# The first three projections on shared x tiles, one more kind of weight split by accumulation, and another order of the last head's value products

## The chip, the cores and the metric

The kernel runs on one core of a Trainium2 chip. The metric is the device time of one launch in microseconds (us). Three runs of the kernel before gave 1087.66, 1087.67 and 1087.76 us, so the median is 1087.67.

## What is computed

One layer of a hybrid encoder: x has 576 rows (512 of a prompt, 64 of a sample) and 1024 columns. A mixer with a gated delta rule and a gated linear attention (4 heads each), a cross attention of 4 heads into 256 memory tokens, and a feed-forward block with a causal convolution are added to x one after the other.

```python
def _mixer(h, p, l, conv_prev, s_a, s_b):
    proj = h @ p['w_in'][l]
    qkv, b_raw, a_raw, z_a, q_b, k_b, v_b, g_lr, z_b, gt_a, gt_b = _split_cols(proj, IN_SIZES)
    qkv, conv_new = _causal_dwconv(qkv, p['conv_a_w'][l], conv_prev)
    ...
    o_a, s_a_new = _gated_delta_chunked(q_a, k_a, v_a, g_a, beta, s_a.astype(f32))
    ...
    merged = jax.nn.sigmoid(gt_a) * y_a + jax.nn.sigmoid(gt_b) * y_b
    return merged @ p['w_o'][l], conv_new, s_a_new, s_b_new

def _cross_attn(h, k, v, w_q, w_o):
    q = (h @ w_q).reshape(B, L, MEM_HEADS, MEM_HD).astype(jnp.float32)
    s = jnp.einsum('blhd,bmhd->bhlm', q, k.astype(jnp.float32)) * (MEM_HD ** -0.5)
    a = jax.nn.softmax(s, axis=-1)
    o = jnp.einsum('bhlm,bmhd->blhd', a, v.astype(jnp.float32)).reshape(B, L, D_MODEL)
    return o.astype(h.dtype) @ w_o

def _trunk(...):
        x = x + _mixer(_rmsnorm(x, p['norm_mix'][l]), ...)
        x = x + _cross_attn(_rmsnorm(x, p['norm_mem'][l]), ...)
        x = x + _conv_ffn(_rmsnorm(x, p['norm_ffn'][l]), ...)
```

Everything is fp32. Outputs are the rows of both requests and the new states.

## The kernel before

**Tiles.** x lies transposed in 8 tiles of 128 features by 576 rows. A weight tile is 128x1024: a block of 128 output columns, its 8 parts of 128 input features side by side. To keep fp32 precision each operand is split into a high half and a low half (the difference), and one product is three matmul passes: high with high, high with low, low with high. `mm3` does this for one x tile: each pass has one matmul of 256 rows and one of 320, six in all. In traces `xh` and `xl` are halves of normed x, `w` holds a weight's halves, `wr` the raw weight as loaded, `ws` a sum of raw blocks, `sm` a PSUM bank.

**Two ways to split a weight.** Either ACT copies the high half (a CAST) and DVE or POOL subtracts to get the low half; or, for tiles called `summed`, ACT writes the negated high half into the low half's place (an ACTIVATE) and a DMA on POOL's queue adds the source to it in place (`w<-wt` from HBM, `w<-ws` from a sum in SBUF). Six weight tiles are in use at a time (three more in a later stage), and four raw ones.

**Products in seven.** The output projection `wo` (and some other weights) is done in pairs of column blocks with seven products for eight (P1, P2, P3, Q4 to Q7) of half-size blocks, each 12 matmuls of 288 columns. P1, P2 and Q4 use one block of the weight; Q5, Q6, P3 and Q7 use sums of blocks (s1 to s4), made by DVE or POOL. `emit_product` (L651) makes the weight of one product, and its flag `summed` (L688) selects the way of the split. After a product DVE adds the bank `sm` to x tiles (`x<-sm`), which frees the bank.

**Order.** Instructions are recorded by coroutines and a planner, class Driver (L251), issues them from one line, L292, engine by engine, by modelled ready times. `X` is a choice between DVE and POOL that the planner makes. So a change of one instruction's kind moves others.

**Start.** `main` (L1686) loads x tiles on SP's queue with the halves of the first weight tiles between them. `WPART` says behind which x tile a half of which raw tile comes. Weights 0 and 1 (q and k of head 0) are laid out together in HBM, so that each half holds both weights' parts for two x tiles. The loop over x tiles multiplies with q and, one tile behind, with k: 16 times `mm3`. Weight 2 (v of head 0) is loaded whole, split by accumulation, and its product follows later by `tile_proj`, after 32 small matmuls with `w` for the gates. Then comes z (`za`). `conv_raw` copies a product from PSUM to the tile u for the convolution.

**Attention.** `c_att` (L1527) does one head: probabilities, transposed and split (`pth`, `ptl`), then two value products of 128 columns each, both copied from PSUM to `ao` by ACT and split by `hl2` into `ach` and `acl`, which the `mo` products use. Between the two value products the coroutine waits for the first `ao`.

Of the kernel before, what the change touches and what calls it, by code (L numbers as in the profile page):

```python
# [10 lines left out]
F32 = mybir.dt.float32  # L11
# [6 lines left out]
P = 128  # L18
# [3 lines left out]
T = TP + TS  # L22
KT = D // P
# [5 lines left out]
RAWB = 4  # L29
# [474 lines left out]
def tile_trunk(ctx, tc, xT, memT, wt, wd, vec, cst, w0, wgate, st_gdn, st_conv, st_gla, st_ffn, ckT, cv,  # L504
# [19 lines left out]
    def nm(s):  # L524
        cnt[0] += 1
        return f"{s}{cnt[0]}"
# [30 lines left out]
    def big():  # L557
        return Pair(sm(), sm())
# [41 lines left out]
    def make(i):  # L600
        fn = unmade.pop(i, None)
        if fn is not None:
            fn()
# [8 lines left out]
    def emit_weight(i, at=0.0):  # L612
        kind, idx = WORDER[i]
        if kind == "*":
            wready[i] = emit_product(i, at, *idx)
            return
        raw = raw_tile()
        n = 1024
        if kind == "dn":
            m, p = idx  # L620
            n = len(PARTS[p]) * 128
            src = wd[m, :, PART0[p] * 128:PART0[p] * 128 + n]
        elif kind in ("outa", "outb"):
            n, c = 512, 512 * (kind == "outb")
            src = wt[WIDX[("out", idx)], :, c:c + 512]
        else:
            src = wt[WIDX[(kind, idx)]]
        DMA(raw[:, :n], src)
        h = w_tile()
        h, lo = (h[:, 0:512], h[:, 512:1024]) if n <= 512 else (h[:], w_tile()[:])  # L630
        summed = kind in SUMMED and (kind, idx) != ("dn", (7, 3))

        def split_():
            if summed:
                split_summed(h[:, :n], lo[:, :n], raw[:, :n], src)
            else:
                A.copy(h[:, :n], raw[:, :n])
                X.tensor_tensor(lo[:, :n], raw[:, :n], f(h[:, :n]), op=ALU.subtract)
            drop(raw[:])

        defer(i, split_, max(drv.ready_at(raw[:, :n]), at - (LEADD if summed else LEADV)))
        wready[i] = (h, lo)
# [8 lines left out]
    def emit_product(i, at, pair, prod):  # L651

        def dram(tile_):
            kind, idx = tile_
            if kind != "dn":
                return wt[WIDX[tile_]], 512
            m, p = idx
            n = len(PARTS[p]) * 64
            return wd[m, :, PART0[p] * 128:PART0[p] * 128 + 2 * n], n

        n = dram(pair[0])[1]
        u = used.setdefault(pair, set())
        if prod == "P1":
            r = halves_of[pair] = []
            for t_ in pair:
                raw = raw_tile()
                src, _ = dram(t_)
                DMA(raw[:, :2 * n], src)
                r += [(raw[:, 0:n], src[:, 0:n]), (raw[:, n:2 * n], src[:, n:2 * n])]
        r = halves_of[pair]  # L670
        (a11, d11), (a12, d12), (a21, _), (a22, d22) = r[:4]

        def total(a, b):
            s_ = slot("ws")
            (X if pair[0][0] in ("wo", "mo") else V).tensor_tensor(s_[:, 0:n], a, b, op=ALU.add)
            return s_[:, 0:n]

        def made(key, a, b):
            if key not in sums:
                sums[key] = total(a(), b())  # L680
            return sums[key]

        sums = sums_of.setdefault(pair, {})
        s1 = lambda: made("s1", lambda: a21, lambda: a22)
        s2 = lambda: made("s2", s1, lambda: a11)
        w = w_tile()
        h, lo = w[:, 0:n], w[:, 512:512 + n]
        summed = prod in ("P1", "P2", "Q4") or prod == "Q5" and n > 256 and pair[0][0] not in ("wo", "dn")  # L688

        def split_():  # L690
            src = {"P1": lambda: a11, "Q5": s1, "Q6": s2, "P3": lambda: made("s4", s2, lambda: a12),
                   "Q7": lambda: made("s3", lambda: a11, lambda: a21), "P2": lambda: a12, "Q4": lambda: a22}[prod]()
            if prod == "Q7":
                made("s4", s2, lambda: a12)
            if summed:
                split_summed(h, lo, src, {"P1": d11, "P2": d12, "Q4": d22}.get(prod, src))
            else:
                A.copy(h, src)
                X.tensor_tensor(lo, src, f(h), op=ALU.subtract)
            u.update({prod} | set(sums))  # L700
            for a, ps in ((a11, {"P1", "s2", "s3", "s4", "P2"}), (a22, {"s1", "s3", "Q4"})):
                if ps <= u:
                    drop(a)

        defer(i, split_, max(drv.ready_at(a11, a22) if prod not in ("P1", "P2") else drv.ready_at(a11), at - (LEADD if summed else LEADV)))
        return h, lo

    def weight(kind, idx, ahead=True, held=False):

        i = wpos[0]  # L710
        assert WORDER[i] == (kind, idx), (WORDER[i], kind, idx)
        wpos[0] = i + 1
        for j in [j for j in wready if j < i - held]:
            drop(*wready.pop(j))
        if i not in wready:
            emit_weight(i)
        make(i)
        if ahead:
            fetch(i + 1, i)
        return wready[i]  # L720
# [32 lines left out]
    cst_t = small_tile([P, NM - 256], F32, tag="cst", name="cst", bufs=1)  # L753
    DMA(vec_t[:, 0:8], vec[:, 0:8])
    x = []
    raws = [wp.tile([P, 1024], F32, tag="raw", name=nm("wr"), bufs=RAWB) for _ in range(2)]
    for t_ in raws:
        keep(drv.rotate("raw", RAWB, t_))

    WPART = {0: (0, 0, 512), 2: (0, 512, 1024), 3: (1, 0, 512), 5: (1, 512, 1024)}  # L760
    for k in range(KT):
        xt = slot("x")
        x.append(xt)
# [28 lines left out]
    def mm3(outs, wh, wl, a, b, k, first, last):  # L792
        ch = wh[:, k * 128:(k + 1) * 128]
        cl = wl[:, k * 128:(k + 1) * 128]
        for o, c in outs:
            PE.matmul(o, ch, a[:, c], start=first, stop=False)
        for o, c in outs:
            PE.matmul(o, ch, b[:, c], start=False, stop=False)
        for o, c in outs:
            PE.matmul(o, cl, a[:, c], start=False, stop=last)  # L800
# [726 lines left out]
    def c_att(hd):  # L1527
# [51 lines left out]
        for j in range(2):  # L1579
            pp, p64 = sm(), sm()  # L1580
            for mt_ in range(2):
                c = slice(256 * mt_ + 128 * j, 256 * mt_ + 128 * j + 128)
                vh_, vl_ = (t[:, c] for t in vp_)
                h, lo = (t[:, 0:TP] for t in pts[mt_])
                PE.matmul(pp, vh_, h, start=mt_ == 0, stop=False)
                PE.matmul(pp, vh_, lo, start=False, stop=False)
                PE.matmul(pp, vl_, h, start=False, stop=mt_ == 1)
                PE.matmul(p64[:, 0:64], vs_[:, c], pst[:, 64 * mt_:64 * mt_ + 64], start=mt_ == 0, stop=mt_ == 1)
            o = slot("ao")
            for c, reg in ((slice(0, TP), pp), (slice(TP, T), p64[:, 0:64])):  # L1590
                A.copy(o[:, c], reg)
            yield [o]
            ao[2 * hd + j] = hl2(o)
            os_.append(o)
            yield
        mops[hd] = {p: cut(ao[2 * hd + i], N1) for i, p in enumerate(("P1", "P2"))}
        drv.done.add(("att", hd))
# [16 lines left out]
    def hl2(src, new=None):  # L1614
        h, lo = [(new or slot)(s, F32R) for s in ("ach", "acl")]
        parts2(h[:, 0:T], lo[:, 0:T], src[:, 0:T])
        return h[:, 0:T], lo[:, 0:T]
# [71 lines left out]
    def main():  # L1689
        acc = slot("acc")  # L1690
        xg = []
        for i in range(2):
            wready[i] = (w_tile()[:], w_tile()[:])

        def wpart(k):
# [35 lines left out]
        DMA(keep_t, cst[:, 0:256])  # L1731
        DMA(cst_t, cst[:, 256:NM])
        drop(*(t_[:] for t_ in raws))
        emit_weight(2)
        make(2)
        DMA(wg_t, wgate)
        DMA(cst_in, st_conv)
        xs = xs_of(xg)
        b0 = []
        (wh0, wl0), (wh1, wl1) = weight("q", 0, False), weight("k", 0, True, True)  # L1740
        first2 = [big(), big()]
        for k in range(KT + 1):
            for i, ps in enumerate(first2):
                j = k - i
                if 0 <= j < KT:
                    wh, wl = (wh0, wl0) if j < 4 else (wh1, wl1)
                    mm3([(ps[:, 0, 0:256], slice(0, 256)), (ps[:, 1, 0:320], slice(256, T))], wh, wl, *xs[j], 2 * (j % 4) + i, j == 0, j == KT - 1)
        raw_u = [conv_raw(ps, V.tensor_copy) for ps in first2]
        for k in range(4, KT):
            sq_act(k)  # L1750
        drv.spawn(c_rstat("n1", [(acc, 0)], 4, True, 0.0))
# [20 lines left out]

        drv.spawn(c_first())

        yield from tile_proj("v", 0, xs, b0)
        u0 = conv_raw(b0[0], A.copy)
        yield from tile_proj("za", 0, xs, b0)
        z0 = slot("z")
        for i, o in pieces(b0[1], z0):
            A.copy(o, i)  # L1780
        yield ("first",)
        def c_gate_operands():
# [709 lines left out]
def pack_inputs(inp):  # L2492
# [13 lines left out]
    for (kind, idx), i in WIDX.items():  # L2506
# [11 lines left out]
        if (kind, idx) in HALVED:  # L2518
            w = np.concatenate([w.reshape(KT, P, P)[0::2], w.reshape(KT, P, P)[1::2]]).reshape(D, P)
        wt[i] = kp(w)  # L2520
    wt[0:2] = wt[0:2].reshape(2, P, 2, 4, P).transpose(2, 1, 3, 0, 4).reshape(2, P, 1024)
    wd = a["w_down"][0].reshape(NJ, P, 8, P)[sum(PARTK, [])].transpose(2, 1, 0, 3).reshape(8, P, NJ * P)

    w0 = np.zeros((D, 32), np.float32)
# [63 lines left out]
```

## Time and profile before

| what | value |
|---|---|
| median of three runs | 1087.67 us |
| the profiled execution, whole | 1090.06 us |
| its span, from the first to the last instruction | 1088.3 us |
| mean granted clock of TensorE | 0.997 |
| matmuls on PE | 8278 records |
| HBM read and written | 158.15 MB, 5.37 MB |

Nothing in this table says which work ends last; for that the page has a chain of work, and the trace has the waits of each engine. In a row of the timeline the first number is the start in us, then duration, engine, line, operation, output<-inputs, shapes and count; in brackets stands the idle time before it and what ended it. A duration of several instructions covers the stretch from the first one's start to the last one's end. A matmul's duration in the trace includes its passage through the array, so consecutive matmuls overlap, and the difference of starts is what one costs. PEld is the load of a weight into the array, which lies beside PE's matmuls. DMA-issuing rows on POOL last as long as the issue; the landing is in the views of the DMA issues.

### The profile page before, as it was taken

Reading aid. Unit: us, or ns where it says so; the run is one execution under the profiler, and the core shown is the slowest. Engines: PE = TensorE matmul, PEld = TensorE weight load, DVE = VectorE, ACT = ScalarE, POOL = GpSimd, SP = SyncE. Lnnn points to the kernel's source line nnn. Section 1 sums busy time; section 2 is a strip of 40 time slices with the busy share of each in tenths; the row PEclk is TensorE's granted clock in tenths of the full one; section 3 lists DMA queues with packets and bytes.
Section 4 is the critical chain, followed back from the end, with each engine's and each line's share of the span. In section 5 each row is a group of like instructions: output and inputs, shape, how many; then the busy total and the mean of one; then the engine's idle time right before and its main releaser. Section 6 shows DMA issues by size and latency. Waiting matters only on the chain.

```text
span 1088.3 us, 21600 instructions
## 1 busy us (share of the span) xinstructions
PE 1077.5 (99%) x8278; PEld 1045.7 (96%) x8278; DVE 749.4 (69%) x1460; ACT 705.9 (65%) x1404; POOL 363.3 (33%) x578
## 2 busy tenths in 40 slices
PE   9999999999999999999999999999999999999997
PEld 7999989998988999999999999999999999999997
DVE  6566844776757586887735766667877776778565
ACT  6675637464647568566755668768876776677645
POOL 1243216134524433123410125444333333332224
PEclk9999999999999999999999999999999999999999
DMA  9666344354136889678684258777788688778934
GB/s 295 145 143 162 70 110 114 76 123 122 43 78 130 213 213 188 246 222 211 174 221 146 49 124 195 175 166 150 166 195 196 146 213 188 168 172 184 201 77 112
DMA packets 68039, 172.00 MB, mean 158 GB/s; under 512 B 7904, under 2 KB 14176, under 8 KB 67936
## 3 DMA queue, kind: packets, MB, share of 16 engines
q0 software_dynamic: 30672, 71.84, 38.2%
q1 hardware_dynamic: 36976, 98.26, 27.7%
q8 instruction: 65, 1.06, 0.4%
q10 hardware_dynamic: 288, 0.52, 0.1%
q14 instruction: 38, 0.31, 0.1%
HBM read 158.15 MB, written 5.37 MB: 150 GB/s over the span
## 4 chain that ended last, share of the span: by engine, by line
PE 97%; DVE 1%; ACT 1%; DMA 0%; issue 0%; SPq 0%; ACTq 0%; DVEq 0%
PE sm L292 97%; DMA x<-xT 0%; DVE ql L292 0%; ACT w L292 0%; DVE w L292 0%; DVE acl L292 0%; DVE ws L292 0%; ACT ach L292 0%; SPq L292 0%; ACT ao L292 0%; DVE q L292 0%; DVE xl L292 0%; ACT xh L292 0%; DVE yo L292 0%; DVE x L292 0%
## 5 line engine op out<-in xcount | busy, mean ns | idle before, releaser
L292 PE MATMUL sm<-xh,w 128*128 128x290 f32 (+3 forms) x2304 | 446.3, 300 | 0.4 <-ACT xh L292 0.3
L292 PEld LDWEIGHTS sm<-xh,w 128*128 128x128 f32 x2304 | 357.2, 189 | 5.4 <-issue 1.7
L292 PE MATMUL sm<-xl,w 128*128 128x290 f32 (+3 forms) x1152 | 270.7, 296 | 0.5 <-DVE xl L292 0.5
L292 POOL DMA_DIRECT2D w<-wt x153 | 135.4, 898 | 372.4 <-ACT w L292 277.4
L292 PE MATMUL sm<-ach,w 128*128 128x256 f32 (+1 forms) x1216 | 230.9, 295 | 2.2 <-DVE x L292 1.7
L292 PEld LDWEIGHTS sm<-xl,w 128*128 128x128 f32 x1152 | 200.9, 189 | 1.0 <-DVE xl L292 1.0
L292 PEld LDWEIGHTS sm<-ach,w 128*128 128x128 f32 x1216 | 189.9, 188 | 3.0 <-ACT w L292 1.9
L292 ACT CAST w<-wr 128x512 fp32r<-128x512 f32 (+5 forms) x207 | 158.7, 769 | 20.8 <-PE sm L292 17.8
L292 ACT ACTIVATE w<-wr 128x512 fp32r<-128x512 f32 (+5 forms) x186 | 142.8, 769 | 20.4 <-PE sm L292 18.7
L292 PE MATMUL sm<-acl,w 128*128 128x256 f32 (+1 forms) x608 | 146.3, 295 | 0.3 <-DVE acl L292 0.3
L292 ACT CAST w<-ws 128x512 fp32r<-128x512 f32 (+1 forms) x132 | 78.4, 603 | 46.8 <-DVE ws L292 26.2
L292 PEld LDWEIGHTS sm<-acl,w 128*128 128x128 f32 x608 | 107.4, 188 | 0.5 <-DVE acl L292 0.5
L292 DVE TENSOR_TENSOR w<-ws,w 128x512 fp32r<-128x512 f32 (+1 forms) x104 | 76.1, 740 | 19.9 <-ACT w L292 17.7
L292 DVE SCALAR_TENSOR_TENSOR fc<-fu,vec,fc 128x578 f32<-128x578 f32 x88 | 70.4, 815 | 3.0 <-ACT fc L292 2.9
L292 PE MATMUL sm<-sh,w 128*128 128x290 f32 x288 | 61.2, 297 | 0.0
L292 DVE TENSOR_TENSOR x<-x,sm 128x320 f32<-128x320 f32 (+3 forms) x95 | 38.7, 437 | 31.4 <-PE sm L292 31.0
L292 POOL DMA_DIRECT2D w<-wd x33 | 29.0, 898 | 64.8 <-ACT w L292 57.9
L292 ACT ACTIVATE fc<-fu,vec 128x578 f32<-128x578 f32 x44 | 38.1, 871 | 17.0 <-POOL fu L292 16.4
L292 PEld LDWEIGHTS sm<-sh,w 128*128 128x128 f32 x288 | 47.5, 189 | 0.0
L292 DVE TENSOR_TENSOR ws<-ws,wr 128x512 f32<-128x512 f32 (+1 forms) x64 | 44.1, 690 | 1.1
L292 PE MATMUL sm<-oh,w 128*128 128x256 f32 (+1 forms) x256 | 44.7, 295 | 0.0
L292 POOL DMA_DIRECT2D w<-ws x27 | 23.6, 873 | 50.4 <-ACT w L292 49.9
(388 smaller groups left out, 1958.1 us busy)
## 6 DMA issues: line engine op xcount, KB each, us to landing
wr<-wt SPq DMA_DIRECT2D x130, 512.0 KB, 5.8
w<-wt POOLq DMA_DIRECT2D x52, 512.0 KB, 6.5
w<-wt POOLq DMA_DIRECT2D x101, 256.0 KB, 6.3
w<-ws POOLq DMA_DIRECT2D x27, 256.0 KB, 5.7
x<-xT SPq DMA_DIRECT2D x16, 288.0 KB, 6.1
wr<-wd SPq DMA_DIRECT2D x8, 448.0 KB, 5.9
w<-wd POOLq DMA_DIRECT2D x8, 448.0 KB, 7.1
wr<-wt SPq DMA_DIRECT2D x12, 256.0 KB, 3.8
```

What stands on the lines that cost most here:

```text
L292: fn(*args, **kw)
```

## The change

There are three edits. First, at the start v joins q and k: three raw tiles come in six halves behind x tiles 0, 1, 2, 3, 5 and 6, the three weights are laid out together in HBM with q, k and v of one x tile next to each other, and each x tile is multiplied with all three before the next. v's product is copied to u directly behind them. Second, `summed` holds also for Q5 of the `wo` pairs but the first, so three subtractions become ACTIVATEs with an accumulating DMA. Third, for head 3 the wait and the split between the two value products are dropped; both splits follow the second.

```diff
--- before.py
+++ after.py
@@ -685,7 +685,7 @@
         s2 = lambda: made("s2", s1, lambda: a11)
         w = w_tile()
         h, lo = w[:, 0:n], w[:, 512:512 + n]
-        summed = prod in ("P1", "P2", "Q4") or prod == "Q5" and n > 256 and pair[0][0] not in ("wo", "dn")
+        summed = prod in ("P1", "P2", "Q4") or prod == "Q5" and n > 256 and (pair[0][0] not in ("wo", "dn") or pair[0][0] == "wo" and pair[0][1])
 
         def split_():
             src = {"P1": lambda: a11, "Q5": s1, "Q6": s2, "P3": lambda: made("s4", s2, lambda: a12),
@@ -753,11 +753,11 @@
     cst_t = small_tile([P, NM - 256], F32, tag="cst", name="cst", bufs=1)
     DMA(vec_t[:, 0:8], vec[:, 0:8])
     x = []
-    raws = [wp.tile([P, 1024], F32, tag="raw", name=nm("wr"), bufs=RAWB) for _ in range(2)]
+    raws = [wp.tile([P, 1024], F32, tag="raw", name=nm("wr"), bufs=RAWB) for _ in range(3)]
     for t_ in raws:
         keep(drv.rotate("raw", RAWB, t_))
 
-    WPART = {0: (0, 0, 512), 2: (0, 512, 1024), 3: (1, 0, 512), 5: (1, 512, 1024)}
+    WPART = {k: (n // 2, 512 * (n % 2), 512 * (n % 2) + 512) for n, k in enumerate((0, 1, 2, 3, 5, 6))}
     for k in range(KT):
         xt = slot("x")
         x.append(xt)
@@ -1589,9 +1589,11 @@
             o = slot("ao")
             for c, reg in ((slice(0, TP), pp), (slice(TP, T), p64[:, 0:64])):
                 A.copy(o[:, c], reg)
-            yield [o]
-            ao[2 * hd + j] = hl2(o)
             os_.append(o)
+            if not (hd == 3) or j:
+                yield [o]
+            for i in (range(2) if j and (hd == 3) else () if (hd == 3) else (j,)):
+                ao[2 * hd + i] = hl2(os_[i])
             yield
         mops[hd] = {p: cut(ao[2 * hd + i], N1) for i, p in enumerate(("P1", "P2"))}
         drv.done.add(("att", hd))
@@ -1689,7 +1691,7 @@
     def main():
         acc = slot("acc")
         xg = []
-        for i in range(2):
+        for i in range(3):
             wready[i] = (w_tile()[:], w_tile()[:])
 
         def wpart(k):
@@ -1731,21 +1733,18 @@
         DMA(keep_t, cst[:, 0:256])
         DMA(cst_t, cst[:, 256:NM])
         drop(*(t_[:] for t_ in raws))
-        emit_weight(2)
-        make(2)
         DMA(wg_t, wgate)
         DMA(cst_in, st_conv)
         xs = xs_of(xg)
         b0 = []
-        (wh0, wl0), (wh1, wl1) = weight("q", 0, False), weight("k", 0, True, True)
-        first2 = [big(), big()]
-        for k in range(KT + 1):
-            for i, ps in enumerate(first2):
-                j = k - i
-                if 0 <= j < KT:
-                    wh, wl = (wh0, wl0) if j < 4 else (wh1, wl1)
-                    mm3([(ps[:, 0, 0:256], slice(0, 256)), (ps[:, 1, 0:320], slice(256, T))], wh, wl, *xs[j], 2 * (j % 4) + i, j == 0, j == KT - 1)
-        raw_u = [conv_raw(ps, V.tensor_copy) for ps in first2]
+        ws = [weight(kd, 0, False, i) for i, kd in enumerate("qkv")]
+        first3 = [big() for _ in range(3)]
+        for k in range(KT):
+            for i, ps in enumerate(first3):
+                n, b = divmod(3 * k + i, 8)
+                mm3([(ps[:, 0, 0:256], slice(0, 256)), (ps[:, 1, 0:320], slice(256, T))], *ws[n], *xs[k], b, k == 0, k == KT - 1)
+        raw_u = [conv_raw(ps, copy) for ps, copy in zip(first3, (V.tensor_copy, V.tensor_copy, A.copy))]
+        fetch(3)
         for k in range(4, KT):
             sq_act(k)
         drv.spawn(c_rstat("n1", [(acc, 0)], 4, True, 0.0))
@@ -1772,11 +1771,10 @@
 
         drv.spawn(c_first())
 
-        yield from tile_proj("v", 0, xs, b0)
-        u0 = conv_raw(b0[0], A.copy)
+        u0 = raw_u[2]
         yield from tile_proj("za", 0, xs, b0)
         z0 = slot("z")
-        for i, o in pieces(b0[1], z0):
+        for i, o in pieces(b0[0], z0):
             A.copy(o, i)
         yield ("first",)
         def c_gate_operands():
@@ -2518,7 +2516,7 @@
         if (kind, idx) in HALVED:
             w = np.concatenate([w.reshape(KT, P, P)[0::2], w.reshape(KT, P, P)[1::2]]).reshape(D, P)
         wt[i] = kp(w)
-    wt[0:2] = wt[0:2].reshape(2, P, 2, 4, P).transpose(2, 1, 3, 0, 4).reshape(2, P, 1024)
+    wt[0:3] = wt[0:3].reshape(3, P, KT, P).transpose(2, 0, 1, 3).reshape(3, 8, P, P).transpose(0, 2, 1, 3).reshape(3, P, 1024)
     wd = a["w_down"][0].reshape(NJ, P, 8, P)[sum(PARTK, [])].transpose(2, 1, 0, 3).reshape(8, P, NJ * P)
 
     w0 = np.zeros((D, 32), np.float32)
```

SP's queue at the start, before and then after (`x` with a number are the x tiles in order, `wr` raw weight tiles in halves of 512 columns):

```order
L292 DMA x_81<-xT 128x576
L292 DMA wr_79<-wt 128x512
L292 DMA x_82<-xT 128x576
L292 DMA x_83<-xT 128x576
L292 DMA wr_79<-wt 128x512
L292 DMA x_84<-xT 128x576
L292 DMA wr_80<-wt 128x512
L292 DMA x_85<-xT 128x576
L292 DMA x_86<-xT 128x576
L292 DMA wr_80<-wt 128x512
L292 DMA x_87<-xT 128x576
L292 DMA x_88<-xT 128x576
```

```order
L292 DMA x_82<-xT 128x576
L292 DMA wr_79<-wt 128x512
L292 DMA x_83<-xT 128x576
L292 DMA wr_79<-wt 128x512
L292 DMA x_84<-xT 128x576
L292 DMA wr_80<-wt 128x512
L292 DMA x_85<-xT 128x576
L292 DMA wr_80<-wt 128x512
L292 DMA x_86<-xT 128x576
L292 DMA x_87<-xT 128x576
L292 DMA wr_81<-wt 128x512
L292 DMA x_88<-xT 128x576
```

Two more halves (the third raw tile) stand among the x tiles, and the halves come one place earlier.

POOL's queue at the `wo` stage, before and then after. Numbers of tiles differ by two or three between the programs: w_6182 in the first fence is w_6184 in the second. The low half of the second pair's Q5 is w_6180 before, which is on DVE (below), and w_6182 after:

```order
L292 DMA w_6121<-wt 128x512
L292 DMA w_6182<-wt 128x512
L292 DMA w_6202<-wt 128x512
L292 TENSOR_TENSOR ws_6223<-ws_6184,wr_6119 128x512
L292 DMA w_6304<-wt 128x512
L292 DMA w_6325<-wt 128x512
```

```order
L292 DMA w_6123<-wt 128x512
L292 DMA w_6184<-wt 128x512
L292 DMA w_6204<-wt 128x512
L292 DMA w_6182<-ws_6183 128x512
L292 DMA w_6328<-wt 128x512
L292 DMA w_6287<-wt 128x512
```

The sum ws<-ws,wr leaves POOL, and a fourth accumulation, from a ws tile, stands behind the three from wt.

DVE's queue at the same place, where x<-sm are the evacuations, before and then after:

```order
L292 TENSOR_TENSOR ws_6181<-wr_6120 128x512
L292 TENSOR_TENSOR ws_6184<-ws_6181,wr_6119 128x512
L292 TENSOR_TENSOR w_6180<-ws_6181,w_6180 128x512
L292 TENSOR_TENSOR w_6183<-ws_6184,w_6183 128x512
L292 SCALAR_TENSOR_TENSOR x_5839<-sm_6185,x_5839 128x288
L292 SCALAR_TENSOR_TENSOR x_5840<-sm_6203,x_5840 128x288
L292 SCALAR_TENSOR_TENSOR x_5839<-sm_6157,x_5839 128x288
L292 TENSOR_TENSOR ws_6242<-wr_6119,wr_6120 128x512
L292 TENSOR_TENSOR w_6222<-ws_6223,w_6222 128x512
```

```order
L292 TENSOR_TENSOR ws_6183<-wr_6122 128x512
L292 TENSOR_TENSOR ws_6186<-ws_6183,wr_6121 128x512
L292 SCALAR_TENSOR_TENSOR x_5841<-sm_6187,x_5841 128x288
L292 SCALAR_TENSOR_TENSOR x_5842<-sm_6205,x_5842 128x288
L292 TENSOR_TENSOR w_6185<-ws_6186,w_6185 128x512
L292 TENSOR_TENSOR ws_6225<-ws_6186,wr_6121 128x512
L292 SCALAR_TENSOR_TENSOR x_5841<-sm_6159,x_5841 128x288
L292 TENSOR_TENSOR w_6224<-ws_6225,w_6224 128x512
```

The subtraction of w_6180 is gone, the two first evacuations stand directly behind the two sums, and the sum that POOL had is third behind them.

PE at the last head, where sm<-pth, ptl, pst are the value product and sm<-ach,w the products of `mo`; the second value product begins in row 5 before and in row 5 after, and what differs is which `ach` product stands ahead of it:

```order
L292 MATMUL sm_8038<-acl_7875,w_7822 128x256
L292 MATMUL sm_8039<-acl_7875,w_7822 128x320
L292 MATMUL sm_8038<-ach_7874,w_7823 128x256
L292 MATMUL sm_8039<-ach_7874,w_7823 128x320
L292 MATMUL sm_8124<-pth_7969,kvh_7942 128x512
L292 MATMUL sm_8124<-ptl_7970,kvh_7942 128x512
L292 MATMUL sm_8124<-pth_7969,kvl_7943 128x512
L292 MATMUL sm_8125<-pst_7983,cvr_7551 128x64
```

```order
L292 MATMUL sm_8043<-acl_7816,w_7828 128x256
L292 MATMUL sm_8044<-acl_7816,w_7828 128x320
L292 MATMUL sm_8043<-ach_7815,w_7829 128x256
L292 MATMUL sm_8044<-ach_7815,w_7829 128x320
L292 MATMUL sm_8118<-pth_7983,kvh_7946 128x512
L292 MATMUL sm_8118<-ptl_7984,kvh_7946 128x512
L292 MATMUL sm_8118<-pth_7983,kvl_7947 128x512
L292 MATMUL sm_8119<-pst_7996,cvr_7579 128x64
```

The six matmuls with ach_7874 (ach_7885 in the changed program) that stood ahead of the second value product stand behind it; ahead of it are now those with ach_7815, which before were the ones ahead of these.

## Prediction

> **What bounds the kernel now.** I read the page first (busy time, then the chain that ended last), then the waits of TensorE, then windows over the stages that the change touches, and only there single instructions.
>
> ```profile
> PE 1077.5 (99%) x8278; PEld 1045.7 (96%) x8278; DVE 749.4 (69%) x1460; ACT 705.9 (65%) x1404; POOL 363.3 (33%) x578
> ...
> PE 97%; DVE 1%; ACT 1%; DMA 0%; issue 0%; SPq 0%; ACTq 0%; DVEq 0%
> ```
>
> TensorE is busy for 1077.5 of 1088.3 us and is 97% of the chain. The change issues as many matmuls as before, so it can only win or lose in waits of TensorE and in the granted clock. The view of the waits names the few that exist:
>
> ```profile
> PE sm L292 <- DVE x L292: 1.7, 1, 1.7
> ...
> PE sm L292 <- DVE xl L292: 0.5, 2, 0.3
> PE sm L292 <- ACT ach L292: 0.5, 1, 0.5
> ...
> PE sm L292 <- DVE ql L292: 0.3, 1, 0.3
> PE sm L292 <- DVE acl L292: 0.3, 1, 0.3
> ```
>
> They lie in three places: the first microseconds (xl, and xh, whose row stands below), the first out-projection pair (DVE x), and the attention (ql, ach, acl). Each part of the change has its own place among them. Together they are 3.6 us, so a larger gain would need the clock too. Times below are those of the profiled execution before the change (span 1088.3, whole execution 1090.06, which is 2.39 over the median of 1087.67); I take the differences as valid for the median as well.
>
> **Part 1, the start: three projections on each x tile.** Windows of one microsecond (span, then busy time of PE, PEld, DVE, ACT and POOL, the granted clock, the DMA share and GB/s), then the timeline:
>
> ```profile
> 6.00:7.00 1.00, 0.80 (x3) 0.37 (x3) 1.00 (x2) 0.30 (x1) 0.00 (x0) 1.00 1.08 373
> 7.00:8.00 1.00, 0.68 (x3) 0.44 (x3) 0.02 (x1) 0.77 (x2) 0.00 (x0) 1.00 1.00 371
> 8.00:9.00 1.00, 0.62 (x3) 0.39 (x3) 0.96 (x2) 1.00 (x3) 0.00 (x0) 1.00 1.05 395
> 9.00:10.00 1.00, 1.00 (x5) 1.00 (x6) 1.00 (x2) 0.87 (x2) 0.00 (x0) 0.57 1.00 381
> 10.00:11.00 1.00, 1.00 (x6) 1.00 (x5) 1.00 (x3) 0.87 (x3) 0.00 (x0) 0.50 1.05 403
> ...
> 12.00:13.00 1.00, 1.00 (x7) 1.00 (x7) 1.00 (x2) 0.87 (x2) 0.00 (x0) 0.72 1.06 369
> ```
>
> ```profile
> 5.88 0.88 PE L292 MATMUL sm<-xh,w 128*128 128x256 f32 x2
> ...
> 7.32 0.43 PE L292 MATMUL sm<-xh,w 128*128 128x256 f32 x2
> 8.06 0.53 PE L292 MATMUL sm<-xh,w 128*128 128x256 f32 x2 [0.31 <-ACT xh L292]
> ...
> 14.79 0.69 PE L292 MATMUL sm<-xh,w 128*128 128x256 f32 x4
> ...
> 15.58 0.69 PE L292 MATMUL sm<-xh,w 128*128 128x256 f32 x4
> ...
> 22.28 2.15 PE L292 MATMUL sm<-x,w 128*32 128x256 f32 x32
> 24.36 0.53 PE L292 MATMUL sm<-xh,w 128*128 128x256 f32 x2
> ```
>
> One tile's product for one projection (six matmuls) takes 15.58 - 14.79 = 0.79 us in the steady part. The 16 of q and k run from 5.88 to 22.28, 16.4 us, against 16 x 0.79 = 12.64: 3.76 are lost. The clock row shows where about half of it went: from 9.1 to 12.6 the clock is at 0.5, so 3.4 us of work done at half rate lose 1.7; the other 2 are waits for x tiles and the work stretched by them. An x tile (128x576 fp32, 288 KB) and half a weight tile (128x512, 256 KB) take 0.75 and 0.67 us at the 371 to 403 GB/s above, so one x tile with its share of weights arrives every 1.4 us. ACT and DVE need about as much:
>
> ```profile
> 9.38 0.78 ACT L292 ACTIVATE xh<-x,vec 128x576 fp32r<-128x576 f32 x1
> 10.07 0.62 ACT L292 CAST w<-wr 128x512 fp32r<-128x512 f32 x1
> ...
> 9.52 0.68 DVE L292 TENSOR_TENSOR w<-wr,w 128x512 fp32r<-128x512 f32 x1
> 10.20 0.82 DVE L292 SCALAR_TENSOR_TENSOR xl<-x,vec,xh 128x576 fp32r<-128x576 f32 x1
> ```
>
> Six weight halves and eight x tiles cost ACT 8 x 0.78 + 6 x 0.62 = 10 us, DVE 8 x 0.82 + 6 x 0.68 = 10.6 us. TensorE before used up a tile in 2 x 0.79 = 1.58, hardly slower than the 1.4 of supply; after, it takes 3 x 0.79 = 2.37. So it is never starved once the first product is done. That first one ends near 7.6 as now (its last two matmuls start at 7.32), since its inputs come in the same order; 23 x 0.79 follow, to 25.75. The same 24 products before cost up to 22.28 for q and k plus 8 for v alone, 8 x 0.79 = 6.32, so 28.6. **Gain 2.85.** It counts the half-clock stretch as gone, because TensorE streams about twice as much in 6 to 9. If it stays, 1.7 of the 2.85 go and 1.2 are left: the two ends. I take the full gain. What hides the rest: v's weights come as two halves among the x tiles (so two loads of 0.67 stand ahead of the loads behind them on SP's queue, whose first user is the 32 matmuls w at 22.28) and no longer as a load of their own with a POOL accumulation; the za weights, now fetched when they are first asked for, find both queues free of these; DVE's two copies and ACT's copy of v stand beside the 32 matmuls w (2.1 us, at 22.28). The gates come 2.85 earlier on TensorE but no earlier on ACT; at worst a wait of 0.3.
>
> **Part 2, the out-projection.** DVE, then POOL, then TensorE where the longest wait is:
>
> ```profile
> 486.34 2.39 DVE L292 TENSOR_TENSOR w<-ws,w 128x512 fp32r<-128x512 f32 x2
> 488.65 1.17 DVE L292 SCALAR_TENSOR_TENSOR x<-sm,x 128x288 f32<-128x288 f32 x3
> ...
> 486.45 1.73 POOL L292 TENSOR_TENSOR ws<-ws,wr 128x512 f32<-128x512 f32 x1
> ...
> 489.61 0.37 PE L292 MATMUL sm<-ach,w 128*128 128x288 f32 x1 [1.75 <-DVE x L292]
> ```
>
> The product P3 of pair 0 writes a bank that the x<-sm evacuation of an earlier one frees, and this stands on DVE behind two subtractions, one of which belongs to the second pair's Q5; both are stretched to 2.39 beside POOL's sum. After, that subtraction is gone from DVE, the sum moves from POOL to DVE behind the evacuations, and these follow the two sums directly. DVE is through the sums at 486.34 and needs 0.4 for each evacuation, while TensorE ends Q6 at 487.7, so **the wait of 1.75 goes**.
>
> The price is that Q5's low half is now made by ACT and an accumulating DMA on POOL, the fourth in a row. The three before it, by their issues (size, microseconds to landing), the whole stage, and the range for this kind:
>
> ```profile
> w<-wt POOLq DMA_DIRECT2D x1, 256.0 KB, 7.5
> ...
> w<-wt POOLq DMA_DIRECT2D x2, 256.0 KB, 8.3
> ...
> w<-wt POOLq DMA_DIRECT2D x1, 256.0 KB, 9.1
> ...
> 480.00:500.00 20.00, 18.25 (x139) 18.05 (x138) 16.11 (x30) 12.91 (x23) 7.18 (x8) 1.00 0.96 269
> ...
> DMA to landing us min/median/max: 3.3/5.7/8.3
> ```
>
> ```profile
> 482.97 1.75 POOL L292 DMA_DIRECT2D w<-wt  x2 [6.12 <-DVE kraw L292]
> 485.57 0.86 POOL L292 DMA_DIRECT2D w<-wt  x1 [0.85 <-ACT w L292]
> ...
> 481.32 1.76 PE L292 MATMUL sm<-hl,w 128*128 128x288 f32 x12
> ...
> 492.88 1.75 PE L292 MATMUL sm<-hl,w 128*128 128x288 f32 x12
> ```
>
> The first was issued at 482.97 and landed 7.5 later (490.5), the third at 485.57 and 9.1 later (494.7), the one between them at about 492.7: one every 2.1 us, with the DMA engines at 0.96. The fourth is issued at 486.4, right behind, and lands at 496.8 by that spacing, or 497.4 if the loads on SP's queue keep more than half; I take 497.1. When is it needed? Pair 0's P1 starts at 481.32 and pair 1's at 492.88: six products with a pause of about 1.9, so 1.6 each. Without the pause pair 1's P1 starts at 490.97, Q5 at 492.57, and its low half is read by the last four of twelve matmuls, from 493.63. **New wait 3.5**; behind it on TensorE stands everything else, on POOL's queue the accumulations of the third pair. Bounds: 0 by the fastest landing of the kind (486.4 + 3.3 = 489.7, in time), 4.6 if the loads on the other queue delay it by one more half of 2.1. In the changed kernel all of it lies 2.85 earlier, supply and demand alike. The wait lies nearest to the rows of its own queue and stage, so I take their value. Q5 of the pairs 2 and 3 have slack, since the same stage falls to a DMA share of 0.72 behind 500.
>
> What the idle time does to the clock: at the start a stretch with TensorE at 0.80, 0.68 and 0.62 was followed by 3.4 us at half clock, while the pause of 1.75 us at 488 was followed by none (the clock reads 1.00 over 480 to 500). A wait of 3.5 is longer than such a stretch is, so I expect the stretch behind it at half clock; about 0.5 of the stretch passes before TensorE resumes, and 2.9 at half rate lose **1.45**. The ends are 0 and 1.7.
>
> The Trainium skill, "TensorE: Matmul & The Clock Gate", section "Part 1: The HAM clock gate (the "warmup" mystery)", says that the clock halves only after at least one idle window of about 3.4 us, and that these windows run freely. The trace agrees with the length (0.57, 0.50, 0.72 over 9 to 13) and differs on "idle": TensorE was working for most of the time ahead of it. By the page a wait of 3.5 would hardly cover a whole window, and the clock would stay.
>
> **Part 3, the attention.**
>
> ```profile
> 620.70 0.38 PE L292 MATMUL sm<-kvh,ql 128*128 128x256 f32 x1 [0.26 <-DVE ql L292]
> ...
> 643.97 0.53 PE L292 MATMUL sm<-ach,w 128*128 128x256 f32 x2 [0.48 <-ACT ach L292]
> 644.76 0.54 PE L292 MATMUL sm<-acl,w 128*128 128x256 f32 x2 [0.26 <-DVE acl L292]
> ```
>
> The second value product of the last head comes six matmuls (0.79 us) earlier and those six stand behind it: the 0.48 goes. The low half waits longer, since the first pair's subtraction now stands behind the second product's: about 0.45 in place of 0.26. Gain 0.29. The 0.26 for ql goes because six more matmuls stand ahead of it in the new order. Sum **0.55**, ends 0 and 0.74.
>
> **Sum.** -2.85 (start) - 1.75 (old wait) - 0.55 (attention) + 3.5 (new wait) + 1.45 (clock) = -0.2: 1087.5.
>
> **Rivals.**
> - *The fourth accumulation lands in time, or up to 1.5 late.* For it speaks the range of the kind (3.3 to 8.3); against it, 9.1 of the nearest. Without any wait -5.15: 1082.5; with 1.5 and no loss of clock 1084.0.
> - *Late, but the clock stays,* since the wait does not fill a window. For it: the pause of 1.75 cost no clock. -5.15 + 3.5: 1086.0. The rule of the Trainium skill quoted above would give this time.
> - *The half clock at the start stays.* TensorE streams more, though still with gaps up to 8. All else as forecast, -0.2 + 1.7: 1089.2.
> - *The accumulating queue bounds the whole stage (slower).* Three subtractions become three more accumulations of 2.1 us, 6.3 of queue time. If the queue holds its spacing past 500, Q5 of pairs 2 and 3 are late too: -5.15 + 6.3 + 1.45 = +2.6: 1090.3. It decides from a spacing of 2.1 with a slack under 2; against it speaks the DMA share of 0.72 there.
> - *The change does not do what it says at the start* would be tiles starved as before; it is in the third case.
>
> **How the numbers follow.** Forecast 0.36, in time 0.30, late at full clock 0.12, half clock at the start 0.08, queue bound 0.14. About 0.2% (2.18 us) is what a measurement of this kernel can tell from no change: faster is below 1085.5, slower above 1089.85. Faster 0.30, same 0.36 + 0.12 + 0.08 = 0.56, slower 0.14. Own range of the forecast: 1086.9 to 1088.1. For 8 in 10 I leave out the better part of a third of the first rival below and most of the last above: 1083.0 to 1089.9.
>
> **What would show it.** Right at the start: the clock at 1.00 over 9 to 13, waits on xl and xh at most once each, and the 32 matmuls w directly behind v's products, near 25.75. In the out-projection: no wait on DVE x, a wait on POOL's or the queue's w of 3 to 4 us, and behind it a window at 0.5. Wrong would be a Q5 without wait (then 1082.5 to 1084), a start still at half clock, or waits at two more Q5.

## The result: slower by half a per cent

| | median, us | runs |
|---|---|---|
| before | 1087.77 | 6 (1087.66 to 1089.29) |
| after | 1093.16 | 6 (1092.48 to 1094.37) |

The ratio is 1.0048, interval 1.0036 to 1.0061, so 5.4 us slower. The forecast was 1087.5 with a range of 1083.0 to 1089.9: the time lies outside it, and the sign is wrong. The profiled execution of the changed kernel took 1093.20 us with a span of 1091.4.

The waits of TensorE in the changed kernel (in total, times, longest):

```profile
PE sm L292 <- DMA w<-ws: 4.7, 1, 4.7
PE sm L292 <- DVE x L292: 1.4, 1, 1.4
...
PE sm L292 <- DVE acl L292: 0.2, 1, 0.2
PE sm L292 <- DVE xl L292: 0.2, 1, 0.2
```

The seven waits of before (xl twice) have shrunk to two of 0.2 and a DVE wait of 1.4 that is not the old one, and a new one of 4.7 stands above them: the accumulation into Q5's low half. Where it is, and what follows it, is seen in windows of the out-projection stage (columns as in the prediction: span, busy time of PE, PEld, DVE, ACT, POOL, the granted clock, the DMA share and GB/s):

```profile
488.00:491.00 3.00, 3.00 (x25) 3.00 (x24) 2.28 (x5) 2.49 (x5) 0.47 (x1) 1.00 1.09 276
491.00:494.00 3.00, 0.37 (x3) 0.13 (x1) 0.00 (x0) 0.78 (x2) 1.25 (x2) 0.96 1.09 302
494.00:496.00 2.00, 0.00 (x0) 0.00 (x0) 0.00 (x0) 0.00 (x0) 0.00 (x0) 0.50 1.06 316
496.00:498.00 2.00, 1.97 (x8) 1.98 (x9) 0.46 (x1) 0.00 (x0) 0.00 (x0) 0.50 1.09 286
498.00:500.00 2.00, 2.00 (x10) 2.00 (x9) 0.00 (x0) 0.00 (x0) 0.00 (x0) 0.50 0.50 94
500.00:502.00 2.00, 2.00 (x14) 2.00 (x14) 1.70 (x3) 1.68 (x4) 0.75 (x1) 0.85 0.01 1
```

TensorE stands still from 491.4 to 496.0 with the DMA engines full, and then works at half clock: 8 to 10 matmuls in a window of two microseconds where 17 are usual. The windows of one microsecond at its two ends say when the clock changed:

```profile
493.00:494.00 1.00, 0.00 (x0) 0.00 (x0) 0.00 (x0) 0.00 (x0) 0.00 (x0) 0.89 1.11 307
...
500.00:501.00 1.00, 1.00 (x7) 1.00 (x7) 0.73 (x2) 0.68 (x2) 0.00 (x0) 0.70 0.01 2
```

A mean of 0.89 is a drop to 0.50 at 493.8, and a mean of 0.70 a return at 500.6. The part of it in which TensorE had work, 496.0 to 500.6, loses half of 4.6, so 2.3 us. The single rows of the same stage, from the timeline:

```profile
484.28 0.86 POOL L292 DMA_DIRECT2D w<-ws  x1 [0.18 <-issue]
...
496.03 1.33 PE L292 MATMUL sm<-ach,w 128*128 128x288 f32 x4 [4.66 <-DMA w<-ws]
```

and the view of the DMA issues for that one (size, microseconds to landing), first of the fourth accumulation, then of the same kind of accumulation at 502.3, issued when the DMA engines were idle:

```profile
w<-ws POOLq DMA_DIRECT2D x1, 256.0 KB, 11.7
...
w<-ws POOLq DMA_DIRECT2D x1, 256.0 KB, 4.2
```

Issued at 484.28, landed at 496.0. The mechanism of the forecast is there, larger than it was sized, and the other losses and gains have to be found beside it. The DVE wait of 1.4 stands in the third pair, while the wait for Q5 was in the second:

```profile
514.34 1.77 POOL L292 TENSOR_TENSOR acc<-acc,sq 128x576 f32<-128x576 f32 x1
...
514.55 2.73 DVE L292 TENSOR_TENSOR w<-ws,w 128x512 fp32r<-128x512 f32 x2 [0.41 <-ACT w L292]
517.20 0.81 DVE L292 SCALAR_TENSOR_TENSOR x<-sm,x 128x288 f32<-128x288 f32 x2
...
517.79 0.37 PE L292 MATMUL sm<-ach,w 128*128 128x288 f32 x1 [1.41 <-DVE x L292]
```

It is the picture of the old wait at 488 again: two subtractions in front of the evacuations, stretched beside a POOL operation.

### The profile page after: what moved, and what is told of

It reads as the page before. It is cut to its first block, busy times and chain, and to the rows that moved or that the text cites. A ratio compares the mean times of both kernels' runs of the same rounds, so it can differ in the third digit from the quotient of the medians.

```text
span 1091.4 us, 21590 instructions
## 1 busy us (share of the span) xinstructions
PE 1077.6 (99%) x8278; PEld 1046.5 (96%) x8278; DVE 749.0 (69%) x1461; ACT 706.5 (65%) x1407; POOL 360.7 (33%) x578
## 4 chain that ended last, share of the span: by engine, by line
PE 96%; DMA 1%; DVE 1%; issue 1%; ACT 0%; POOL 0%; SPq 0%; POOLq 0%; ACTq 0%
PE sm L292 96%; DMA w<-ws 1%; DMA wr<-wt 0%; DVE ql L292 0%; POOL w L292 0%; DVE ws L292 0%; DVE acl L292 0%; ACT ao L292 0%; ACT ach L292 0%; DVE w L292 0%; ACT w L292 0%; SPq L292 0%; DVE yo L292 0%; DVE q L292 0%; ACT qh L292 0%
## 5 line engine op out<-in xcount | busy, mean ns | idle before, releaser
L292 DVE TENSOR_TENSOR w<-ws,w 128x512 fp32r<-128x512 f32 (+1 forms) x101 | 72.2, 723 | 19.0 <-ACT w L292 17.2
L292 POOL DMA_DIRECT2D w<-ws x30 | 26.7, 891 | 51.6 <-ACT w L292 50.7
```

The lines of the kernel that those rows point to most:

```text
L292: fn(*args, **kw)
```

## The experiments

Every kernel was timed against the kernel before on the same chip; times are medians.

**The kernel before, profiled again.** No edit.

> The kernel before, profiled once more. The profiled execution of it that was read for the prediction took 1090.06 us, 2.4 over the median of the others, with half clock from 9.1 to 12.6 us. Theory A (the profile's losses are those of every run): a profile like it, half clock at the start, 1087.7 in the timed runs. Rival B (the windows of the clock lie elsewhere from run to run): a profile without half clock at the start or with another span, 1 to 2.5 us below 1088.3.

Measured: 1087.85 (11 runs), profiled execution 1087.71 with a span of 1085.9, 2.3 below the span that was read for the prediction. Its first microseconds:

```profile
6.00:7.00 1.00, 0.80 (x3) 0.48 (x3) 0.90 (x2) 1.00 (x3) 0.00 (x0) 1.00 0.98 379
7.00:8.00 1.00, 0.81 (x7) 0.70 (x5) 1.00 (x2) 1.00 (x3) 0.00 (x0) 1.00 1.03 403
8.00:9.00 1.00, 1.00 (x8) 0.90 (x8) 1.00 (x3) 0.88 (x2) 0.00 (x0) 1.00 1.07 416
9.00:10.00 1.00, 1.00 (x10) 1.00 (x9) 1.00 (x2) 0.92 (x2) 0.00 (x0) 1.00 1.04 403
10.00:11.00 1.00, 1.00 (x10) 1.00 (x9) 1.00 (x3) 0.96 (x2) 0.00 (x0) 1.00 1.04 385
```

and from its timeline:

```profile
6.12 0.89 PE L292 MATMUL sm<-xh,w 128*128 128x256 f32 x2 [0.81 <-ACT w L292]
...
19.95 2.15 PE L292 MATMUL sm<-x,w 128*32 128x256 f32 x32
```

No half clock, and from 8 us on no gap. The 16 products of q and k take 19.95 - 6.12 = 13.83 us, where the first profile had 16.4. Of the 3.76 that seemed to be lost there, 1.2 are left, and these the change keeps: alone, its 24 products take 26.03 - 5.92 = 20.1 us against 24 x 0.79 = 19.0 (rows below).

The bad start begins with the second x tile. Its load was issued at 2.1 in both profiles and landed late in the first one (first fence: the profile that was read for the prediction, second fence: this one; size and microseconds to landing):

```profile
x<-xT SPq DMA_DIRECT2D x1, 288.0 KB, 5.1
```

```profile
x<-xT SPq DMA_DIRECT2D x1, 288.0 KB, 4.3
```

The tiles behind it are about 0.8 later too. When the half clock begins the same matmuls are 0.8 later than here, when it ends 2.3, and so they stay. Why that tile came late is not known. Rival B holds: the profile that was read was an execution with a bad start. Of the 27 timed runs of the kernel before that go with this one, 24 took 1087.5 to 1088.7 and three 1089.5 to 1089.8; whether those three had such a start was not seen.

**The first part alone:** all the hunks of the diff in `main`, the raw tiles and the layout, and neither of the others.

> The first part alone (q, k and v share the first x tiles). Theory A: -2.4 us, as the two profiles show it up to 230 us, 1085.3. Rival B (most timed runs of the kernel before have no half clock at the start): -0.7, so 1087.0.

Measured 1088.01 against 1087.83 (ratio 1.0001, interval 0.9992 to 1.0010). Nothing is gained, even less than rival B said. The first product and the matmuls behind the 24 products in its profile:

```profile
5.92 0.88 PE L292 MATMUL sm<-xh,w 128*128 128x256 f32 x2
...
26.03 2.15 PE L292 MATMUL sm<-x,w 128*32 128x256 f32 x32
```

The loss of 1.1 to 1.2 at the start is the same with two products for each x tile and with three. Sharing the tiles among three was to starve TensorE less, but two do not starve it either.

**The second part alone:** the `summed` line.

```diff
-        summed = ... prod == "Q5" and n > 256 and pair[0][0] not in ("wo", "dn")
+        summed = ... prod == "Q5" and n > 256 and (pair[0][0] not in ("wo", "dn") or pair[0][0] == "wo" and pair[0][1])
```

> The second part alone (Q5 of the wo pairs 2 to 4 split by accumulation). Theory A, from the two profiles: -1.75 (old wait gone) +4.7 (wait for the accumulation) +2.3 (half clock behind it) +1.4 (DVE wait one pair later) = +6.7, 1094.4. Rival C (the wait came only because the start shifted supply against demand): no wait for the accumulation beyond 2 us, +0.5, 1088.2.

Measured 1095.35 against 1087.83 (ratio 1.0066, interval 1.0053 to 1.0078), +7.5, in its profile a wait of 4.9 for the accumulation and 1.4 for DVE. The clock drops here too, for 3.4 us from 496.5:

```profile
496.00:497.00 1.00, 0.56 (x2) 0.56 (x3) 0.00 (x0) 0.00 (x0) 0.00 (x0) 0.76 1.09 309
...
499.00:500.00 1.00, 1.00 (x6) 1.00 (x6) 0.00 (x0) 0.00 (x0) 0.00 (x0) 0.53 0.07 12
```

The second part alone is slower than the whole change. Theory A holds, 0.8 too small, and rival C falls: the wait does not need the new start.

**The first and third parts, without the second.**

> The first and third parts without the second. Theory A: -2.4 - 0.7 = -3.1, 1084.6, with the wait of 1.75 for DVE x still there. Rival B: -0.7 - 0.7, 1086.3.

Measured 1087.61 against 1087.83 (0.9997, interval 0.9988 to 1.0006). The size of theory A, 3.1, fails by its start term, and rival B's 1.4 is also more than there is. In its profile the attention gains 0.8, and a slow drift in the feed-forward block behind it takes that back (end of the next section).

**The third part alone:** the hunk in `c_att`.

> The third part alone (last head's value products without a split between them). From the waits of the two profiles: -0.26 (ql), -0.48 (ach), +-0.1 (acl), so -0.4 to -0.7: 1087.2 to 1087.4. Rival (the small steps are lost again behind it): 1087.8.

Measured 1087.14 against 1087.94 (0.9992, interval 0.9983 to 1.0001): 0.8 less, though the interval just includes no change. Its waits show what it does: of before's ql 0.3, ach 0.5 and acl 0.3 these are left:

```profile
PE sm L292 <- DVE ql L292: 0.3, 1, 0.3
PE sm L292 <- DVE acl L292: 0.2, 1, 0.2
```

The 0.48 for ach is gone. The ql wait stays, so the third part is not what ends it; in the whole change, where the second part moves the stage ahead of it, it is under 0.2. In the trace the same matmuls start 0.1 later than in the second profile of before ahead of the second value product (636) and 0.65 earlier behind it (640), a gain of 0.8.

**Q5's accumulation one place and two places forward.** The edit changes the queue's order by issuing other accumulations later, so this is a dose: fourth (the change), third, second. The lines that set the delay (cut), first for the third place, then for the second:

```diff
-        self.put(issue, [(issuer.dma_start, (out, in_), dict(accum_op=ALU.add))])
+        self.put(issue + after, [(issuer.dma_start, (out, in_), dict(accum_op=ALU.add))])
...
+                split_summed(..., 3.0 if (pair[0], prod) in ((("wo", 0), "Q4"), (("wo", 2), "P2")) else 0.0)
...
+                split_summed(..., {(("wo", 0), "Q4"): 4.5, (("wo", 2), "P2"): 3.0}.get((pair[0], prod), 0.0))
```

> The whole change, with Q5's accumulation from ws moved one place ahead on POOL's queue (third instead of fourth, P2's behind it); nothing else moves. Theory Q (the place in the queue makes it late, one every 2.1 to 2.5 us): it lands about 2.3 earlier, the wait of 4.7 becomes 2.2 to 2.5, and the half clock behind it shrinks or goes: -2.3 to -4.7 against the whole change (1093.2), so 1088.5 to 1090.9. Rival S (an accumulation from SBUF is itself slow in this stage, 11.7 us wherever it stands): the wait stays, 1093.

> The same with Q5's accumulation second, ahead of pair 0's Q4 and of P2. Theory Q: it lands another 2 us earlier, its wait is 0 to 1; Q4's, now third, is needed near 493 and may be 0.5 to 1 late: 1086.7 to 1088.5. Rival S: 1093.

Measured 1090.19 and 1088.47 against 1087.84 (ratios 1.0019, interval 1.0009 to 1.0028, and 1.0007, interval 0.9998 to 1.0017). The row of the waits and the landing, third and then second:

```profile
PE sm L292 <- DMA w<-ws: 2.5, 1, 2.5
...
w<-ws POOLq DMA_DIRECT2D x1, 256.0 KB, 9.5
```

```profile
PE sm L292 <- DMA w<-ws: 1.7, 1, 1.7
...
w<-ws POOLq DMA_DIRECT2D x1, 256.0 KB, 8.7
```

| place in the queue | to landing | wait | profiled execution | median |
|---|---|---|---|---|
| fourth | 11.7 | 4.7 | 1093.20 | 1093.16 |
| third | 9.5 | 2.5 | 1089.25 | 1090.19 |
| second | 8.7 | 1.7 | 1088.61 | 1088.47 |

Theory Q holds from fourth to third: 2.2 us earlier for one place, and rival S falls. That it is the place and not the source shows in the accumulation that is fourth instead. It comes from HBM, and in the kernel with the third place it took as long as Q5's had:

```profile
w<-wt POOLq DMA_DIRECT2D x1, 256.0 KB, 11.5
```

Over the three kernels and from either source the second took 8.7 to 9.2, the third 9.5 to 10.2 and the fourth 11.5 to 12.3.

From third to second only 0.8 more, and the wait of 0 to 1 that theory Q had for this place did not come. In both kernels the accumulation is issued at 484.2, since POOL waits until ACT has written the negated high half. That it then still takes 8.7 behind a single other one was not followed; the loads that SP has in flight are the likely reason. So even second it waits 1.7, as long as the wait of 1.75 that the change removed. None of the three places wins.

The ten runs of the kernel with the third place fall into two groups: four of 1088.79 to 1089.25 (the profiled one, without half clock, is among them) and six of 1090.08 to 1090.81. The mean clock was 0.997 to 0.998 in the six and 0.998 to 1.000 in the four. That a wait of 2.5 drops the clock in some executions and not in others would explain this, but it is not shown: only the profiled one was seen in detail.

**Zeros while it waits.** 36 matmuls of zeros into Q5's bank, ahead of the four that need the low half, so that TensorE streams during the wait.

```diff
+            if (pair[0], prod) == (("wo", 2), "Q5"):
+                for _ in range(36):
+                    drv.hold(drv.pe.matmul, 0.0, (o, wh[:, 0:128], zero_r.unsqueeze(1).broadcast_to([P, 9, 32])), dict(start=False, stop=False, skip_group_check=True))
```

> The whole change, with 36 matmuls of zeros added to Q5's bank ahead of the four that wait for the low half (4.7 us of TensorE's time at full rate), so that TensorE streams while it waits. Theory K (idle time costs the clock): the clock stays at 1.00 and the 2.3 us behind the wait come back, 1090.9. Rival (what follows is slow for its weights, not its clock): 1093.

Measured 1091.86, 1.3 less than the change. The stage's windows:

```profile
494.00:496.00 2.00, 2.00 (x17) 2.00 (x16) 0.00 (x0) 0.00 (x0) 0.00 (x0) 1.00 1.09 317
496.00:498.00 2.00, 2.00 (x17) 2.00 (x16) 0.46 (x1) 0.00 (x0) 0.00 (x0) 1.00 1.10 264
498.00:500.00 2.00, 2.00 (x17) 2.00 (x16) 1.87 (x4) 1.86 (x4) 0.86 (x1) 1.00 0.20 37
```

The clock stays at 1.00 and 17 matmuls pass in two microseconds, so theory K holds for the clock. Of the 2.3 only 1.3 come back. Of the rest, 0.6 is a wait for another accumulation that appeared near 680, and 0.3 is lost because the zeros end at 495.8 and the low half had landed at 495.5.

**The second part for the third pair only** (`pair[0][1] == 4` in place of `pair[0][1]`).

> The whole change, with the second part only for the third wo pair (columns 4 and 5). Theory Q: Q5 of the second pair is subtracted on DVE as before, so no 4.7 and no half clock, but the old wait of 1.75 is back: 1087.6; with the wait for DVE near 516 (1.4) as in the whole change, 1089. Rival (the splitting by accumulation costs wherever it is used): 1090 or more.

Measured 1087.07 against 1087.84 (0.9992, interval 0.9982 to 1.0002). No wait for an accumulation, the old DVE wait of 1.7 is back, the one near 516 is not there. The 0.8 under before is what the third part gives alone, so the third pair's accumulation neither costs nor gains anything that shows. Splitting by accumulation does not cost wherever it is used; it costs for the second pair's Q5, which is needed 7 us after it can be issued. The fourth pair's was not tried by itself, so which of the two makes the DVE wait of 1.4 near 516 is not told apart.

**The sums of the `wo` weights kept on DVE**, first without the second part, then with it for the third pair only.

```diff
-            (X if pair[0][0] in ("wo", "mo") else V).tensor_tensor(s_[:, 0:n], a, b, op=ALU.add)
+            (X if pair[0][0] in ("mo",) else V).tensor_tensor(s_[:, 0:n], a, b, op=ALU.add)
```

> The first and third parts without the second, and the sums of the wo weights kept on DVE, so that POOL's one sum (1.73 us) no longer runs beside DVE's two subtractions. Theory P (the old wait of 1.75 is made by DVE being stretched to 2.4 for two subtractions of 0.69 beside a POOL sum): the subtractions take 1.3 to 1.4, the wait shrinks to 0.4 to 0.8, 1086.6. Rival (the queue of work ahead of the evacuation makes it, not the stretching): the wait stays over 1.3, 1087.5.

> The whole change with the second part only for the third wo pair, and the wo sums on DVE. Theory P: 1 us below the same without this (1087.1), 1086.1. Rival: 1087.1.

Measured 1088.19 against 1087.94 (1.0003, interval 0.9994 to 1.0011), and 1086.85 against 1087.94 (0.9989, interval 0.9980 to 0.9998). DVE at the place of the old wait, without and then with POOL's sum beside it (the kernel of the first and third parts):

```profile
483.79 1.53 DVE L292 TENSOR_TENSOR w<-ws,w 128x512 fp32r<-128x512 f32 x2
485.23 0.82 DVE L292 SCALAR_TENSOR_TENSOR x<-sm,x 128x288 f32<-128x288 f32 x2
```

```profile
484.12 2.38 DVE L292 TENSOR_TENSOR w<-ws,w 128x512 fp32r<-128x512 f32 x2
486.43 1.18 DVE L292 SCALAR_TENSOR_TENSOR x<-sm,x 128x288 f32<-128x288 f32 x3
```

The waits for DVE in the kernel without the second part, then in the one with it for the third pair:

```profile
PE sm L292 <- DVE x L292: 2.2, 2, 1.3
```

```profile
PE sm L292 <- DVE x L292: 0.9, 1, 0.9
```

Two subtractions take 1.53 instead of 2.38, and the wait there is 0.87 instead of 1.73. So the stretching made half of the old wait: theory P is right in kind, with a little less than it had said (1.3 to 1.4, and a wait of 0.4 to 0.8). It does not hold for the time. In the first kernel a second wait for DVE, of 1.3, appears near 520. In the second there is none, and it is the fastest of all, 1.1 us under before; but against the kernel with POOL's sum (1087.07) that is 0.2 to 0.3 and not the 1 us that theory P gave. In the traces it gains 0.9 on that kernel in this stage and gives 0.4 of it back in the feed-forward block, for a reason that was not followed.

## Why the prediction was wrong, step by step

| term | predicted | in the profiles of after and of before, taken again |
|---|---|---|
| start | -2.85 | -0.1 (timed alone: +0.2) |
| old DVE wait | -1.75 | -1.75 |
| attention, third part | -0.55 | -0.8 |
| order of the work ahead of it | 0 | -0.3 |
| wait for Q5's accumulation | +3.5 | +4.7 |
| half clock behind it | +1.45 | +2.3 |
| DVE wait in a later pair | 0 | +1.4 |
| sum | -0.2 | +5.5 |

The terms of the attention are changes in how much later the same matmul starts in the changed kernel: 6.5 at 560, 6.1 at 636, 5.3 at 640. The step of 0.8 at 637 stands in the kernel of the third part alone too, and part of the 0.3 ahead of it in that of the second part alone (6.5 to 6.3). The others are waits and the half-clock stretch above. The spans differ by 1091.4 - 1085.9 = 5.5, the medians by 5.4. The forecast missed by 5.65: 2.75 of it is the start, 3.45 the out-projection (1.2 for the wait, 0.85 for the clock, 1.4 for the later DVE wait), and the attention made up 0.55.

- **The step that failed is "Gain 2.85", with "I take the differences as valid for the median as well".** The profiled execution was 2.39 us above the median; I noted it and went on. That excess lay almost wholly in the first 13 us: half clock and late x tiles, which the second profile of the same kernel does not have. The gain was worked out of the disturbance. The second profile loses 1.2 at the start, and the change does not remove that either: it gains 0.1 there, and nothing when timed alone. The rate at which x tiles come, 1.4 us each against 1.58 of work, stood in the same paragraph and said so: two products per tile were enough. (1.4 is the time of a tile with a whole half of a weight; with four halves among eight tiles it is 1.1, and the landings in the second profile are 1.1 apart.) That most executions have no half clock at the start should have been a rival by itself, with the excess as its evidence. With a start of -0.1 the sum would have been +2.55, 1090.3, and the out-projection would still have been 2.9 short.
- **The accumulation: right mechanism, sized too small.** Forecast were 10.7 us from issue to landing and a wait of 3.5; measured 11.7 and 4.7. The spacing of 2.1 that I took from three landings was 2.2 to 3.1 in the changed kernel. Of the 1.2 that the wait was longer, 1.0 is the landing; the other 0.2 is that Q5's low half was needed a little sooner after its issue (7.1 us) than worked out (7.2). The dose shows that the place in the queue costs and not the source: the fourth took 11.5 to 12.3 from either. That the load beside it costs is argued from the 4.2 with idle engines; the load alone was not varied. "If the loads on the other queue delay it" was the bound of 4.6, and that is about where it ended.
- **The clock: right, sized too small.** I counted one stretch of 3.4 us at half clock; it was 6.8 long, 493.8 to 500.6. The Trainium skill, "TensorE: Matmul & The Clock Gate", section "Part 1: The HAM clock gate (the "warmup" mystery)", has the clock halve after one idle window of about 3.4 us and return after a busy one. The return agrees: TensorE began again at 496.0, and the clock came back at 500.6, at the end of the first step of 3.4 us (497.2 to 500.6) that it filled. The drop is earlier than the rule has it: at 493.8, when TensorE had stood still for 2.4 us and not for 3.4. In the profile of the second part alone it fits, since TensorE had stood still in nearly all of the 3.4 us ahead of 496.5. The rival that the Trainium skill's rule gave, no drop, did not come.
- **"Q5 of the pairs 2 and 3 have slack" was right, but not what mattered there.** Their accumulations came in time (4.2 to landing at 502.3). What was missed is a wait of 1.4 on DVE in the third pair: the new order moved two subtractions beside a POOL operation and ahead of evacuations. I had read the stretching at 488 as a thing that goes and did not ask where else it may arise. The rival "the accumulating queue bounds the whole stage" forecast a slower kernel, +2.6, for another reason, late Q5 of the pairs 2 and 3; that it had the sign right is luck.
- **"The wait of 1.75 goes"** was right in kind and size. **The attention** was right for the 0.48, and its size of 0.55 came near the 0.8 partly by luck: the low half was to wait 0.45 and waited 0.2, and the 0.26 for ql was to go by the third part, which alone leaves it.

Part of a point stays open: the second part alone costs 7.5, the whole change 5.4. By the spans of the profiles it is 7.1 against 5.5. Of these 1.6, 0.8 is the third part's step at 637, which the second part alone does not have. About 0.5 lies in a slow drift in the feed-forward block behind 640, where the second part alone falls back by 0.7 against before and the whole change by 0.2. Such a drift stands between several of these profiles: the kernel of the first and third parts is 0.8 ahead of before at 720 and 0.15 behind it at the end, which is where its gain went. Its cause was not followed.

## What to carry to other kernels

Before a stall is priced from a profile, compare that execution's time with the timed median: an excess as large as the gain in view says that the profile shows a bad execution, and a second profile settles it. A low half made by an accumulating DMA is free only where its landing, counted by its place in the queue under the load of that stage, is earlier than its use; a subtraction of 0.7 us is cheaper than a wait of 4.7 and the clock behind it. When an operation is moved off an engine, look at which pairs of operations on DVE and POOL now run at the same time.

## What the runs showed of the hardware that was not expected

- Of four accumulations of 256 KB issued within 4 us, with the DMA engines at a share of 1.0 to 1.1 from 486 until the landing, the last landed 11.7 us after its issue; issued with the engines idle the same kind took 4.2.
- The clock changes in steps of 3.4 us: the half-clock stretches were 3.4 long in the first profile of before, 6.8 in the changed kernel and 3.4 with the second part alone. In the changed kernel it dropped at 493.8 with the pause beginning at 491.4, so TensorE was busy for three tenths of the 3.4 us ahead of the drop, and it returned 6.8 us later. With the second part alone the pause began at 491.5 and the drop came at 496.5, one such step after 493.1; the step that ended at 493.1 was about half busy and no drop followed. Busy time alone does not decide: in the first profile of before TensorE was busy for 0.80, 0.68 and 0.62 of the microseconds ahead of the drop at 9.1, though with 3 matmuls in each where 10 are usual. No threshold comes out of these runs. Pauses of 1.7 were followed by none in any profile of this stage. Matmuls of zeros held the clock at 1.00.
- Two DVE subtractions of 128x512 took 2.38 us beside one POOL sum and 1.53 without it.
